# Down projection of a transformer layer, second phase: the last five inner steps done product by product, with their split weights kept in free slots

## The chip, the cores and the metric

The kernel runs on one core of one Trainium2 chip. The metric is device time in microseconds (us) of one execution. The kernel before was timed three times; its median is 942.09 us (941.8 to 942.45).

## The reference

One layer on 512 tokens of width 1024: a gated mixer of four branches, cross attention to 256 memory tokens, and a convolutional feed-forward part. The change touches the last matrix product, the down projection of the feed-forward part, and the place where its weights are prepared:

```python
def conv_ffn(h, w_up, conv_w, conv_b, w_down):
    up = causal_dwconv(h @ w_up, conv_w, conv_b)
    g, val = jnp.split(up, 2, axis=-1)
    return (jax.nn.gelu(g) * val) @ w_down          # (512 x 2816) @ (2816 x 1024)

    h = rms_norm(x, g[5])
    y = conv_ffn(h, ffn_w_up[l], ffn_conv_w[l], ffn_conv_b[l], ffn_w_down[l])
    x = x + rms_norm(y, g[6])                       # the layer's output
```

## The kernel before

All products are done in float32 precision by splitting each operand into a rounded high part and a low part: three matmuls (high by high, high by low, low by high) in `mm3`, lines 127 to 130. So every weight tile is loaded by SP's queue into a `raw` buffer (4 of them, used in turn), cast on ACT into `whi` (line 75) and subtracted on DVE into `wlo` (line 76), in `load_unit`. There are 4 buffers each of `whi` and `wlo`; a cast into one waits until PE has read what was in it four units earlier. `prefetch` keeps such units two ahead of their use. `unit_kept` does the same split into general slots (70 tiles of 128x512, handed out by `get` and returned by `put`), so that the split weights stay as long as wanted and wait for no `whi` buffer; a unit of 1024 columns takes two casts and two subtractions of 512 columns there.

The down projection is done as a 2 by 2 block product with seven products in place of eight. Token blocks are the two halves of the 512 tokens (each two tiles of 128), and the inner dimension is split in two halves of 11 tiles; an **inner step** i takes tile i of each half. The block sums of `w_down` that this needs are made on the chip earlier: `sums_load` (line 637) loads four quarters of one step on POOL's queue, `sums` (line 644) adds them on DVE and stores them to `wsum` in HBM. These run every third step of the gate loop (line 663 on), and the last two in the loop for the keys (`kT`, lines 800 to 803).

The down projection has two phases. The first (line 1081 on) runs four of the seven products over 11 steps; the second (line 1126 on) runs the other three, here called p3, p7 and p4 by the names of their PSUM banks, each for two token tiles. In the second phase a step needs two weight units: `wb` (512 columns of `w_down`, called **b** below, with the step's number) for p3, and `wz` (1024 columns of `wsum`, called **z**) for p7 and p4. A step is 3 products by 2 token tiles by 3 matmuls, 18 matmuls of 512 columns. For steps 0 to 8 the 18 matmuls are issued together. Steps 9 and 10 are held back and done **product by product**: p3 of tile 0 for both steps, then p3 of tile 1, then p7, then p4, and after each such block of 6 matmuls DVE and ACT finish what it made possible:

- after p3 of tile t: a subtraction (L1149), square and row sum on ACT (L724), gain (L1050), root (L732, L733), then `finish`: two scale-and-add (L1055) and two stores (L1056);
- after p7: a subtraction (L1154), a scale-and-add (L1155), square, gain;
- after p4 of tile t: an addition (L1159), square, gain, root, and `finish` of tile t + 2.

The operands of step i + 1 are made by `second_b` (line 1116) while step i runs. A list scheduler sets the order of each engine's instructions from the order of the program; each engine then works in order.

Of the kernel before, what the change touches and what calls it, by code (L numbers as in the profile page):

```python
# [8 lines left out]
F32 = mybir.dt.float32  # L9
F32R = mybir.dt.float32r  # L10
# [6 lines left out]
P = 128  # L17
S = 512
# [8 lines left out]
LOOK = 2  # L27

# [10 lines left out]
def tile_trunk(ctx: ExitStack, tc: tile.TileContext, a: dict, out: bass.AP):  # L39
# [21 lines left out]
    def put(*ts):  # L61
        for t in ts:
            free.append(held.pop(id(t))[0])
# [32 lines left out]
    for i in range(NP):  # L96
        plan += [(a["w_down"][NP + i][:, S:2 * S], S), (wsum[NP + i], 1024)]
# [536 lines left out]

    quarters = {}

    def sums_load(i):
        q = [[get("wq") for _ in R2] for _ in R2]
        for r in R2:
            for c in R2:  # L640
                gpsimd.dma_start(q[r][c], a["w_down"][c * NP + i][:, r * S:(r + 1) * S])
        quarters[i] = q

    def sums(i):
        (b11, b12), (b21, b22) = quarters.pop(i)
# [4 lines left out]
        gpsimd.dma_start(wsum[i][:, 0:S], b11)  # L650
        gpsimd.dma_start(wsum[i][:, S:2 * S], b22)
        gpsimd.dma_start(wsum[NP + i][:, 0:S], b21)
        gpsimd.dma_start(wsum[NP + i][:, S:2 * S], b12)
        put(b11, b12, b21, b22)

# [3 lines left out]
    for ki, kb in enumerate(order):  # L659
        for m in range(KT):  # L660
# [46 lines left out]
    LO, HI = slice(0, 256), slice(256, S)  # L707
# [45 lines left out]
    yt = [[None, None] for _ in T4]  # L753
# [250 lines left out]
    def pair_up(i):  # L1004
        g0, g1 = g[2 * i], g[2 * i + 1]
        hi, lo = get("gh", F32R), get("gl", F32R)
        for j, t in enumerate((g0, g1)):
            c = slice(j * 256, (j + 1) * 256)
            scalar.copy(hi[:, c], t[:, LO])
            vector.tensor_tensor(lo[:, c], t[:, LO], hi[:, c].bitcast(F32), op=ALU.subtract)  # L1010
        vector.tensor_sub(g1[:, LO], g0[:, LO], g1[:, LO])
        vector.tensor_sub(g0[:, LO], g0[:, LO], g0[:, HI])
        vector.tensor_sub(g0[:, HI], g1[:, HI], g0[:, HI])
        vector.tensor_add(g1[:, LO], g1[:, LO], g0[:, HI])
        gp1[i] = (hi, lo)
# [30 lines left out]
    def down_post(t, c):  # L1046
        n5.square(yt[t][c], t, c)
        if c == (1 if t < 2 else 0):
            n5.add(t, t + 1)
        vector.tensor_tensor(yt[t][c], yt[t][c], g6[c], op=ALU.mult)  # L1050

    def finish(t):
        n5.root(t, t + 1)
        for c in range(2):
            vector.scalar_tensor_tensor(yt[t][c], yt[t][c], n5.col(t), xt[t][c], op0=ALU.mult, op1=ALU.add)  # L1055
            sync.dma_start(out[t][:, HALF[c]], yt[t][c])  # L1056
        put(*yt[t])


    def product(ps, x, off, w, first, last, ts=(0, 1)):  # L1060
        for t in ts:
            tt = slice(off + t * P, off + (t + 1) * P)
            mm3(ps[t], (x[0][:, tt], x[1][:, tt]), w, first, last)

    T2 = (0, 1)
    ops = {}

    def second_a(i):
        g0, g1 = g[2 * i], g[2 * i + 1]
        r = get("r2")  # L1070
        hi, lo = get("sh", F32R), get("sl", F32R)
        vector.tensor_add(r[:, HI], g0[:, LO], g1[:, HI])
        scalar.copy(hi[:, LO], g0[:, HI])
        scalar.copy(hi[:, HI], r[:, HI])
        vector.tensor_sub(lo[:, LO], g0[:, HI], hi[:, LO].bitcast(F32))
        vector.tensor_sub(lo[:, HI], r[:, HI], hi[:, HI].bitcast(F32))
        put(r)
        ops[i] = (hi, lo)

    p1, p2, p6, p5 = ([bank(tag, "dn") for _ in T2] for tag in "BBCA")  # L1080
    second_a(0)
    held_a = []
    for i in range(NP):
        wa, ws = unit(), unit()
        if i + 1 < NP:
            second_a(i + 1)
        f, l = i == 0, i == NP - 1
        todo = [(p1, gp1[i], 0, wa(0, S), f, l), (p2, gp1[i], 256, wa(S, 2 * S), f, l),
                (p6, ops[i], 256, ws(S, 2 * S), f, l), (p5, ops[i], 0, ws(0, S), f, l)]
        if i < NP - 2:  # L1090
            for p in todo:
                product(*p)
            put(*gp1[i], *ops.pop(i))
        else:
            held_a.append(todo)
    d0, d1 = [get("d0") for _ in T2], [get("d1") for _ in T2]
    for n in range(4):
        for t in T2:
            for todo in held_a:
                product(*todo[n], ts=(t,))  # L1100
        for t in T2:
            if n == 0:
                yt[t][0] = get("yt")
                scalar.copy(yt[t][0], p1[t])
            elif n == 2:
                vector.tensor_sub(d0[t], p6[t], yt[t][0])
                vector.tensor_add(yt[t][0], yt[t][0], p2[t])
                down_post(t, 0)
                if t == 0:
                    scalar.activation(warm, n5.ss[:, 0:1], AF.Sqrt, scale=0.0, bias=epsc)  # L1110
            elif n == 3:
                vector.tensor_sub(d1[t], d0[t], p5[t])
    for i in (NP - 2, NP - 1):
        put(*gp1[i], *ops.pop(i))

    def second_b(i):
        g0, g1 = g[2 * i], g[2 * i + 1]
        ah, al = get("sh", F32R), get("sl", F32R)
        bh, bl = get("sh", F32R), get("sl", F32R)
        scalar.copy(ah, g1)  # L1120
        vector.tensor_sub(al, g1, ah.bitcast(F32))
        scalar.copy(bh[:, LO], g0[:, LO])
        vector.tensor_sub(bl[:, LO], g0[:, LO], bh[:, LO].bitcast(F32))
        put(g0, g1)
        ops[i] = (ah, al), (bh, bl)

    p3, p7, p4 = ([bank(tag, "dn") for _ in T2] for tag in "BBC")
    second_b(0)
    held_b = []
    for i in range(NP):  # L1130
        wb, wz = unit(), unit()
        if i + 1 < NP:
            second_b(i + 1)
        f, l = i == 0, i == NP - 1
        ga, gb = ops[i]
        todo = [(p3, ga, 0, wb(0, S), f, l), (p7, gb, 0, wz(S, 2 * S), f, l), (p4, ga, 256, wz(0, S), f, l)]
        if i < NP - 2:
            for p in todo:
                product(*p)
            put(*ga, *gb)  # L1140
        else:
            held_b.append(todo)
    for n in range(3):
        for t in T2:
            for todo in held_b:
                product(*todo[n], ts=(t,))
            if n == 0:
# [93 lines left out]
```

## Time and profile before

| | |
|---|---|
| median of 3 runs | 942.09 us |
| the profiled execution's own time | 941.86 us |
| its span, first to last instruction | 940.0 us |
| PE (matmul) busy | 922.4 us, 98% |
| DVE busy | 606.7 us, 65% |
| ACT busy | 441.1 us, 47% |
| chain that ended last | PE 94%, DVE 3%, ACT 2% |

The table is read from the bottom: the chain of work that ended last is PE's for 94% of the span, so that in most places only fewer matmuls or fewer gaps between them would shorten the time. The 3% of DVE and 2% of ACT say that somewhere PE is not what is waited for.

### The profile page before, as it was taken

What the parts mean: (1) busy time and instruction counts of PE and PEld (TensorE: products, weight loads), DVE (VectorE), ACT (ScalarE), POOL (GpSimd) and SP (SyncE); (2) the same over time, 40 slices, a digit from 0 to 9 for tenths busy, and PEclk for the clock granted to TensorE, in tenths of its full rate; (3) what the DMA queues carried; (4) which work ended last, traced back from release to release, by engine and by line L of the source; (5) the groups of instructions that cost most, each with busy time, mean ns of one, the idle gap of its engine ahead of it and who ended that gap; (6) DMA issues with size and microseconds to landing.
All of it is one profiled execution on the core that took longest, in us unless ns stands there. A gap on an engine that the chain in (4) does not pass through costs nothing.

```text
span 940.0 us, 12070 instructions
## 1 busy us (share of the span) xinstructions
PE 922.4 (98%) x4534; PEld 776.9 (83%) x4534; DVE 606.7 (65%) x940; ACT 441.1 (47%) x707; POOL 56.0 (6%) x117
## 2 busy tenths in 40 slices
PE   8999999999999999999999999999999999999994
PEld 7888888888888888889888888988888888888883
DVE  5877569645665566757544845486666666697847
ACT  7836336422342233456433737453443443465642
POOL 1100022401110000300000000000000000000000
PEclk9999999999999999999999999999999999999997
DMA  9432255835564524745522330133322322355552
GB/s 333 141 130 101 101 190 178 290 133 181 192 227 136 195 94 155 241 140 179 180 90 77 125 112 1 48 110 95 107 90 98 104 90 93 120 178 181 166 191 90
DMA packets 43563, 133.67 MB, mean 142 GB/s; under 512 B 6240, under 2 KB 7152, under 8 KB 43504
## 3 DMA queue, kind: packets, MB, share of 16 engines
q1 hardware_dynamic: 36288, 109.81, 35.5%
q0 software_dynamic: 7072, 23.09, 7.1%
q8 instruction: 35, 0.57, 0.2%
q14 instruction: 24, 0.20, 0.1%
q10 hardware_dynamic: 144, 0.00, 0.0%
HBM read 119.25 MB, written 13.63 MB: 141 GB/s over the span
## 4 chain that ended last, share of the span: by engine, by line
PE 94%; DVE 3%; ACT 2%; DMA 0%; issue 0%; SPq 0%; DVEq 0%; ACTq 0%
PE up L130 8%; PE up L128 8%; PE up L129 8%; PE gate L128 6%; PE gate L129 6%; PE gate L130 6%; PE win L128 4%; PE win L129 3%; PE win L130 3%; PE dn L129 3%; PE dn L128 3%; PE dn L130 3%; PE br L128 2%; PE mo L128 2%; PE q L128 2%; PE q L130 2%
## 5 line engine op out<-in xcount | busy, mean ns | idle before, releaser
L76 DVE TENSOR_TENSOR wlo<-raw,whi 128x1024 fp32r<-128x1024 f32 (+1 forms) x181 | 214.3, 1189 | 155.5 <-ACT whi L75 155.0
L75 ACT CAST whi<-raw 128x1024 fp32r<-128x1024 f32 (+1 forms) x181 | 185.1, 1026 | 276.0 <-issue 78.9
L128 PE MATMUL up<-h3h,whi 128*128 128x512 f32 (+1 forms) x368 | 138.2, 375 | 0.0
L129 PE MATMUL up<-h3l,whi 128*128 128x512 f32 (+1 forms) x368 | 138.1, 375 | 0.0
L130 PE MATMUL up<-h3h,wlo 128*128 128x512 f32 (+1 forms) x368 | 138.1, 375 | 0.0
L128 PE MATMUL gate<-xgh,whi 128*128 128x512 f32 x256 | 99.9, 390 | 0.0
L130 PE MATMUL gate<-xgh,wlo 128*128 128x512 f32 x256 | 99.7, 389 | 0.0
L129 PE MATMUL gate<-xgl,whi 128*128 128x512 f32 x256 | 99.6, 389 | 0.0
L129 PEld LDWEIGHTS up<-h3l,whi 128*128 128x128 f32 x368 | 69.3, 188 | 12.6
L128 PEld LDWEIGHTS up<-h3h,whi 128*128 128x128 f32 x368 | 69.3, 188 | 12.5
L130 PEld LDWEIGHTS up<-h3h,wlo 128*128 128x128 f32 x368 | 69.3, 188 | 12.3
L550 DVE SCALAR_TENSOR_TENSOR c<-up,par,c 128x511 f32<-128x511 f32 (+1 forms) x88 | 65.1, 745 | 1.3
L128 PE MATMUL win<-xgh,whi 128*128 128x512 f32 x144 | 57.2, 397 | 0.0
L128 PEld LDWEIGHTS gate<-xgh,whi 128*128 128x128 f32 x256 | 48.1, 188 | 10.0
L130 PEld LDWEIGHTS gate<-xgh,wlo 128*128 128x128 f32 x256 | 48.1, 188 | 10.0
L130 PE MATMUL win<-xgh,wlo 128*128 128x512 f32 x144 | 56.3, 391 | 0.0
L129 PEld LDWEIGHTS gate<-xgl,whi 128*128 128x128 f32 x256 | 48.1, 188 | 9.8
L129 PE MATMUL win<-xgl,whi 128*128 128x512 f32 x144 | 56.1, 390 | 0.0
L356 DVE TENSOR_TENSOR sg<-gate,rb0s 128x512 f32<-128x512 f32 x32 | 22.0, 688 | 44.5 <-PE gate L130 44.3
L128 PE MATMUL dn<-whi,sh 128*128 128x512 f32 x110 | 42.8, 389 | 0.0
L129 PE MATMUL dn<-wlo,sh 128*128 128x512 f32 x110 | 42.8, 389 | 0.0
L130 PE MATMUL dn<-whi,sl 128*128 128x512 f32 x110 | 42.8, 389 | 0.0
(376 smaller groups left out, 1736.3 us busy)
## 6 DMA issues: line engine op xcount, KB each, us to landing
raw<-in_w_up SPq DMA_DIRECT2D x44, 512.0 KB, 3.4
raw<-in_w_gate SPq DMA_DIRECT2D x32, 512.0 KB, 4.1
wq<-in_w_down POOLq DMA_DIRECT2D x44, 256.0 KB, 3.9
wsum<-wq POOLq DMA_DIRECT2D x44, 256.0 KB, 3.3
raw<-wsum SPq DMA_DIRECT2D x22, 512.0 KB, 3.6
raw<-in_w_in SPq DMA_DIRECT2D x18, 512.0 KB, 3.9
raw<-in_w_down SPq DMA_DIRECT2D x11, 512.0 KB, 4.3
raw<-in_w_br SPq DMA_DIRECT2D x8, 512.0 KB, 3.5
```

The lines of the kernel that those rows point to most:

```text
L75: scalar.copy(hi[:, :n], raw[:, :n])
L76: vector.tensor_tensor(lo[:, :n], raw[:, :n], hi[:, :n].bitcast(F32), op=ALU.subtract)
L128: tensor.matmul(ps, lhsT=w[0], rhs=x[0], start=first, stop=False)
L129: tensor.matmul(ps, lhsT=w[0], rhs=x[1], start=False, stop=False)
L130: tensor.matmul(ps, lhsT=w[1], rhs=x[0], start=False, stop=last)
L356: vector.tensor_tensor(t, ps, rb0s, op=ALU.mult)
L550: vector.scalar_tensor_tensor(dst[:, s:S], src[:, 0:S - s], pc(wname, (taps - 1 - s) * stride + off), dst[:, s:S], op0=ALU.mult, op1=ALU.add)
```

## The change

`HOLD = 5` steps of the second phase, 6 to 10 in place of 9 and 10, are held back and done product by product, so that a block has 15 matmuls. Their weights can't stay in the four `whi` buffers so long, so they are loaded by `unit_kept` into slots. `plan` ends 5 steps earlier; when step 5 is taken, the kept units of steps 6 and 7 are asked for, and each further step asks for one more. The two phases move into a function `seven`. The casts and subtractions of one small operand now share one slot (`sb`). The sums of `w_down` are started every second gate step from the sixth on, so that all 11 are done in the gate loop and none in the loop for the keys.

```diff
+HOLD = 5
-    for i in range(NP):
+    for i in range(NP - HOLD):
         plan += [(a["w_down"][NP + i][:, S:2 * S], S), (wsum[NP + i], 1024)]
...
+    def pair_b(g0, g1):
+        ah, al, b = get("sh", F32R), get("sl", F32R), get("sb", F32R)
+        scalar.copy(ah, g1)
+        vector.tensor_sub(al, g1, ah.bitcast(F32))
+        scalar.copy(b[:, LO], g0[:, LO])
+        vector.tensor_sub(b[:, HI], g0[:, LO], b[:, LO].bitcast(F32))
...
+    def seven(n, first, opa, opb, wua, wub, ha, hb, ready):
...
+            if i < n - hb:
+                for p in todo:
+                    product(*p)
+                put(ah, al, b)
+            else:
+                held.append(todo)
+                free_later += [ah, al, b]
+        for k in range(3):
+            for t in T2:
+                for todo in held:
+                    product(*todo[k], ts=(t,))
+                if k == 0:
+                    yt[t][1] = get("yt")
+                    vector.tensor_sub(yt[t][1], d1[t], bks[0][t])
+                    ready(t, 1, True)
...
+    def sums_step(load=True):
+        if len(summing) > 1 or (summing and not sumq):
+            sums(summing.pop(0))
+        if load and sumq:
+            summing.append(sumq.pop(0))
+            sums_load(summing[-1])
...
-            step = ki * KT + m - 5
-            if step >= 0 and step % 3 == 0:
-                sums_load(step // 3)
-            if step >= 2 and step % 3 == 2:
-                sums(step // 3)
+            if ki * KT + m >= 5 and (ki * KT + m - 5) % 2 == 0:
+                sums_step()
...
-        if m in (2, 4):
-            sums(8 + m // 2)
-        if m in (0, 2):
-            sums_load(9 + m // 2)
+        sums_step()
...
+    def w_second(i):
+        if i < NP - HOLD:
+            return unit(), unit()
+        b, ts = unit_kept(a["w_down"][NP + i][:, S:2 * S], S)
+        z, tz = unit_kept(wsum[NP + i])
+        kept_down[i] = ts + tz
+        return b, z
+
+    kept_at = ahead(lambda j: w_second(NP - HOLD + j), HOLD, 1)
+
+    def w_later(i):
+        if i >= NP - HOLD:
+            return kept_at(i - NP + HOLD)
+        w = w_second(i)
+        if i == NP - HOLD - 1:
+            kept_at(0)
+        return w
+
+    seven(NP, gp1, ahead(lambda i: pair_a(g[2 * i], g[2 * i + 1]), NP, 1),
+          ahead(lambda i: pair_b(g[2 * i], g[2 * i + 1]), NP, 1),
+          lambda i: (unit(), unit()), w_later, 2, HOLD, down_ready)
```

Three places show how the engines' orders move. First PE, right after the last matmul of step 5. Before (`dn_7395` and `dn_7396` are the banks of p3 for token tiles 0 and 1, `dn_7397` that of p7 for tile 0; `whi_7600` is b of step 6, `whi_7606` its z; `sh` and `sl` are the token operand):

```order
L128 MATMUL dn_7395<-whi_7600,sh_7611 128x512
L129 MATMUL dn_7395<-wlo_7601,sh_7611 128x512
L130 MATMUL dn_7395<-whi_7600,sl_7612 128x512
L128 MATMUL dn_7396<-whi_7600,sh_7611 128x512
L129 MATMUL dn_7396<-wlo_7601,sh_7611 128x512
L130 MATMUL dn_7396<-whi_7600,sl_7612 128x512
L128 MATMUL dn_7397<-whi_7606,sh_7613 128x512
```

Now, from the fourth held step on (`sv_7395` and `sv_7396` are p3 of tiles 0 and 1; `kwh` and `kwl` are the kept high and low parts: 7595 and 7596 of step 6, 7611 and 7612 of step 7, 7682 and 7683 of step 9, 7705 and 7706 of step 10):

```order
L129 MATMUL sv_7395<-kwh_7682,sh_7696 128x512
L130 MATMUL sv_7395<-kwl_7683,sh_7696 128x512
L131 MATMUL sv_7395<-kwh_7682,sl_7697 128x512
L129 MATMUL sv_7396<-kwh_7595,sh_7625 128x512
L130 MATMUL sv_7396<-kwl_7596,sh_7625 128x512
L129 MATMUL sv_7395<-kwh_7705,sh_7719 128x512
L131 MATMUL sv_7396<-kwh_7595,sl_7626 128x512
L129 MATMUL sv_7396<-kwh_7611,sh_7650 128x512
L130 MATMUL sv_7396<-kwl_7612,sh_7650 128x512
L130 MATMUL sv_7395<-kwl_7706,sh_7719 128x512
L131 MATMUL sv_7395<-kwh_7705,sl_7720 128x512
```

PE went from step to step and used each weight for two tiles at once; now it goes through p3 of tile 0 for steps 6 to 9, and the scheduler has put two matmuls of tile 1 ahead of step 10's first and three ahead of its second.

Second, ACT at the same place, from the last weight unit in a `whi` buffer (`whi_7563`, z of step 5) on. It was one cast of b and one of z per step; now (z of step 6 is `kwh_7601` and `kwh_7605`, of step 7 7617 and 7621, of step 8 7665 and 7669, of step 9 7688 and 7692; `sb_7721` and `sh_7696` are token operands):

```order
L665 CAST sh_7696<-c_6671 128x512
L76 CAST whi_7563<-raw_7562 128x1024
L118 CAST kwh_7601<-raw_7599 128x512
L118 CAST kwh_7605<-raw_7599 128x512
L118 CAST kwh_7611<-raw_7609 128x512
L118 CAST kwh_7617<-raw_7615 128x512
L118 CAST kwh_7621<-raw_7615 128x512
L118 CAST kwh_7659<-raw_7657 128x512
L118 CAST kwh_7665<-raw_7663 128x512
L118 CAST kwh_7669<-raw_7663 128x512
L118 CAST kwh_7682<-raw_7680 128x512
```

The kept casts stand in one run behind z of step 5, in the order of the steps.

Third, the end of DVE's order. Before:

```order
L1154 TENSOR_TENSOR d_925_7329<-d_925_7329,dn_7398 128x512
L1155 SCALAR_TENSOR_TENSOR d_923_7327<-d_923_7327,dn_7398 128x512
L1159 TENSOR_TENSOR d_922_7326<-d_922_7326,dn_7399 128x512
L1050 TENSOR_TENSOR d_925_7329<-d_925_7329,gain_6877 128x512
L1159 TENSOR_TENSOR d_923_7327<-d_923_7327,dn_7400 128x512
L728 TENSOR_TENSOR rs_n_6881<-ss_n_6880 128x1
L1050 TENSOR_TENSOR d_922_7326<-d_922_7326,gain_6876 128x512
L728 TENSOR_TENSOR rs_n_6881<-ss_n_6880 128x1
L1050 TENSOR_TENSOR d_923_7327<-d_923_7327,gain_6876 128x512
L733 RECIPROCAL rs_n_6881<-rs_n_6881 128x1 x2
L1055 SCALAR_TENSOR_TENSOR d_922_7326<-d_922_7326,rs_n_6881,xt_3157 128x512
L1055 SCALAR_TENSOR_TENSOR d_924_7328<-d_924_7328,rs_n_6881,xt_3158 128x512
```

Now (`sv_7399` and `sv_7400` are p4 of tiles 0 and 1, as `dn_7399` and `dn_7400` were):

```order
L739 TENSOR_TENSOR d_922_7326<-d_922_7326,sv_7399 128x512
L845 TENSOR_TENSOR rs_n_6881<-ss_n_6880 128x1
L1153 TENSOR_TENSOR d_922_7326<-d_922_7326,gain_6876 128x512
L850 RECIPROCAL rs_n_6881<-rs_n_6881 128x1
L1159 SCALAR_TENSOR_TENSOR d_922_7326<-d_922_7326,rs_n_6881,xt_3189 128x512
L1159 SCALAR_TENSOR_TENSOR d_924_7328<-d_924_7328,rs_n_6881,xt_3190 128x512
L739 TENSOR_TENSOR d_923_7327<-d_923_7327,sv_7400 128x512
L845 TENSOR_TENSOR rs_n_6881<-ss_n_6880 128x1
L1153 TENSOR_TENSOR d_923_7327<-d_923_7327,gain_6876 128x512
L850 RECIPROCAL rs_n_6881<-rs_n_6881 128x1
L1159 SCALAR_TENSOR_TENSOR d_923_7327<-d_923_7327,rs_n_6881,xt_3191 128x512
L1159 SCALAR_TENSOR_TENSOR d_925_7329<-d_925_7329,rs_n_6881,xt_3192 128x512
```

The finishing of the two last tiles was interleaved; now tile 2 is finished altogether before the addition that waits for PE's last block.

## Rows read from the trace of the kernel before

**Rows 1.** The page of the profile: busy time of the engines, and the chain that ended last by engine.

```profile
PE 922.4 (98%) x4534; PEld 776.9 (83%) x4534; DVE 606.7 (65%) x940; ACT 441.1 (47%) x707; POOL 56.0 (6%) x117
PE 94%; DVE 3%; ACT 2%; DMA 0%; issue 0%; SPq 0%; DVEq 0%; ACTq 0%
```

**Rows 2.** Busy time by stretches at the end; the columns are the stretch, its length, busy us and count of PE, PEld, DVE, ACT and POOL, the granted clock of TensorE as a share of full speed, the busy share of the DMA engines, GB/s.

```profile
900.00:920.00 20.00, 20.00 (x90) 16.58 (x89) 9.02 (x10) 8.12 (x10) 0.00 (x0) 1.00 0.46 156
...
926.00:928.00 2.00, 1.33 (x6) 0.76 (x5) 2.00 (x5) 0.00 (x0) 0.00 (x0) 1.00 0.70 262
928.00:930.00 2.00, 0.00 (x0) 0.00 (x0) 2.00 (x4) 0.45 (x1) 0.00 (x0) 1.00 0.71 262
930.00:932.00 2.00, 0.00 (x0) 0.00 (x0) 2.00 (x6) 1.05 (x5) 0.00 (x0) 0.60 0.00 0
932.00:934.00 2.00, 0.00 (x0) 0.00 (x0) 1.88 (x6) 1.14 (x4) 0.00 (x0) 0.50 0.00 0
```

**Rows 3.** The chain that ended last, where it leaves PE and its last piece: start us, us, what.

```profile
918.95 0.24 PE dn L130
...
919.21 1.06 ACT whi L75
920.30 1.22 DVE wlo L76
921.52 0.61 DVE yt L1149
...
934.98 1.32 DVE d L1055 x2
```

**Rows 4.** The last matmuls on PE in order of time: start us, us, engine, line, operation, out<-in.

```profile
926.49 0.39 PE L128 MATMUL dn<-whi,sh 128*128 128x512 f32 x1
...
926.95 0.39 PE L130 MATMUL dn<-whi,sl 128*128 128x512 f32 x1
```

**Rows 5.** DVE, ACT and SP's queue at the end in order of time (neighbours of one kind are merged, with their count); in brackets the idle time before and what ended it.

```profile
928.83 0.68 DVE L1154 TENSOR_TENSOR d<-d,dn 128x512 f32<-128x512 f32 x1
...
931.23 0.68 DVE L1159 TENSOR_TENSOR d<-d,dn 128x512 f32<-128x512 f32 x1
...
931.94 0.63 ACT L724 ACTIVATE sq<-d 128x512 f32<-128x512 f32 x1 [0.48 <-DVE d L1159]
...
932.70 0.16 DVE L728 TENSOR_TENSOR rs_n<-ss_n 128x1 f32<-128x1 f32 x1
...
933.38 0.21 DVE L733 RECIPROCAL rs_n<-rs_n 128x1 f32<-128x1 f32 x2
933.57 2.74 DVE L1055 SCALAR_TENSOR_TENSOR d<-d,rs_n,xt 128x512 f32<-128x512 f32 x4
934.35 2.32 SPq L1056 DMA_DIRECT2D out_y<-d  x4
```

**Rows 6.** ACT in the second phase in order of time: casts of 512 and 1024 columns.

```profile
888.14 0.62 ACT L75 CAST whi<-raw 128x512 fp32r<-128x512 f32 x1
888.66 0.62 ACT L1120 CAST sh<-c 128x512 fp32r<-128x512 f32 x1
...
894.73 1.05 ACT L75 CAST whi<-raw 128x1024 fp32r<-128x1024 f32 x1 [2.10 <-PE dn L130]
...
898.81 1.05 ACT L75 CAST whi<-raw 128x1024 fp32r<-128x1024 f32 x1 [2.10 <-PE dn L130]
...
919.21 1.05 ACT L75 CAST whi<-raw 128x1024 fp32r<-128x1024 f32 x1 [2.09 <-PE dn L130]
```

**Rows 7.** DVE in the second phase in order of time: two neighbouring subtractions of 512 columns.

```profile
883.61 0.68 DVE L76 TENSOR_TENSOR wlo<-raw,whi 128x512 fp32r<-128x512 f32 x1
884.22 0.68 DVE L1121 TENSOR_TENSOR sl<-c,sh 128x512 fp32r<-128x512 f32 x1
```

**Rows 8.** SP's queue in the second phase: the transfers of b of step 6, z of step 6 and b of step 7.

```profile
893.68 0.74 SPq L74 DMA_DIRECT2D raw<-in_w_down  x1
897.07 0.33 SPq L74 DMA_DIRECT2D raw<-wsum  x1
897.67 0.33 SPq L74 DMA_DIRECT2D raw<-in_w_down  x1
```

**Rows 9.** Transfers of `raw` tiles by issue, each line: what, count, KB each, us from issue to landing. First the spread of all from 880 to 925 us, then those issued from 886.9 to 889 us (two), then those issued from 888.9 to 890 us (two, while the others were under way).

```profile
DMA to landing us min/median/max: 2.7/3.4/4.3
...
raw<-wsum SPq DMA_DIRECT2D x1, 512.0 KB, 3.3
raw<-in_w_down SPq DMA_DIRECT2D x1, 256.0 KB, 3.3
...
raw<-wsum SPq DMA_DIRECT2D x1, 512.0 KB, 4.2
raw<-in_w_down SPq DMA_DIRECT2D x1, 256.0 KB, 4.3
```

**Rows 10.** The gate stage: DVE's addition of `w_down` quarters and the reading of a gate bank behind it, PE's first matmul that uses that bank again, and the stretch of the stage in which the DMA engines are fullest (columns as in Rows 2).

```profile
190.95 0.69 DVE L646 TENSOR_TENSOR wq<-wq,wq 128x512 f32<-128x512 f32 x1 [6.47 <-DMA wq<-in_w_down]
191.56 0.68 DVE L356 TENSOR_TENSOR sg<-gate,rb0s 128x512 f32<-128x512 f32 x1
...
194.06 0.39 PE L128 MATMUL gate<-xgh,whi 128*128 128x512 f32 x1
...
167.00:174.00 7.00, 7.00 (x35) 5.86 (x34) 5.57 (x8) 3.76 (x5) 2.89 (x6) 1.00 0.94 303
```

More of the change, by code (lines that the diff above doesn't have):

```diff
@@ new lines, in product @@
+    def product(ps, x, off, w, first, last, ts=T2):
+        for t in ts:
+            tt = slice(off + t * P, off + (t + 1) * P)
+            mm3(ps[t], (x[0][:, tt], x[1][:, tt]), w, first, last)
+    def seven(n, first, opa, opb, wua, wub, ha, hb, ready):
+        bks = [[bank(tag, "sv") for _ in T2] for tag in "BBCA"]
+        held, free_later = [], []
+        for i in range(n):
+            wa, ws = wua(i)
+            a, e = first[i], opa(i)
+            f, l = i == 0, i == n - 1
+            todo = [(bks[0], a, 0, wa(0, S), f, l), (bks[1], a, 256, wa(S, 2 * S), f, l),
+                    (bks[2], e, 256, ws(S, 2 * S), f, l), (bks[3], e, 0, ws(0, S), f, l)]
+            if i < n - ha:
+                for p in todo:
+                    product(*p)
+                put(*a, *e)
+            else:
+                held.append(todo)
+                free_later += [*a, *e]
+        d0, d1 = [get("d0") for _ in T2], [get("d1") for _ in T2]
+        for k in range(4):
+            for t in T2:
+                for todo in held:
+                    product(*todo[k], ts=(t,))
+            for t in T2:
+                if k == 0:
+                    yt[t][0] = get("yt")
+                    scalar.copy(yt[t][0], bks[0][t])
+                elif k == 2:
+                    vector.tensor_sub(d0[t], bks[2][t], yt[t][0])
+                    vector.tensor_add(yt[t][0], yt[t][0], bks[1][t])
+                    ready(t, 0, False)
+                elif k == 3:
+                    vector.tensor_sub(d1[t], d0[t], bks[3][t])
+        put(*free_later)
+        bks = [[bank(tag, "sv") for _ in T2] for tag in "BBC"]
+        held, free_later = [], []
+        for i in range(n):
+            wb, wz = wub(i)
+            ah, al, b = opb(i)
+            f, l = i == 0, i == n - 1
+            todo = [(bks[0], (ah, al), 0, wb(0, S), f, l), (bks[1], (b[:, LO], b[:, HI]), 0, wz(S, 2 * S), f, l),
+                    (bks[2], (ah, al), 256, wz(0, S), f, l)]
+            if i < n - hb:
+                for p in todo:
+                    product(*p)
+                put(ah, al, b)
+            else:
+                held.append(todo)
+                free_later += [ah, al, b]
+        for k in range(3):
+            for t in T2:
+                for todo in held:
+                    product(*todo[k], ts=(t,))
+                if k == 0:
+                    yt[t][1] = get("yt")
+                    vector.tensor_sub(yt[t][1], d1[t], bks[0][t])
+                    ready(t, 1, True)
+                elif k == 1:
+                    yt[t + 2][1] = d1[t]
+                    vector.tensor_sub(d1[t], d1[t], bks[1][t])
+                    vector.scalar_tensor_tensor(d0[t], d0[t], -1.0, bks[1][t], op0=ALU.mult, op1=ALU.add)
+                    ready(t + 2, 1, False)
+                else:
+                    yt[t + 2][0] = d0[t]
+                    vector.tensor_add(d0[t], d0[t], bks[2][t])
+                    ready(t + 2, 0, True)
+        put(*free_later)
@@ L1044, in tile_trunk, with down_ready @@
     n5 = TokNorm("n5")
-    def down_post(t, c):
+    def down_ready(t, c, last):
         n5.square(yt[t][c], t, c)
-        if c == (1 if t < 2 else 0):
+        if last:
             n5.add(t, t + 1)
         vector.tensor_tensor(yt[t][c], yt[t][c], g6[c], op=ALU.mult)
[L1052 to L1057, printed above, removed]
@@ L1060, in product @@
[L1060 to L1078, printed above, removed]
@@ L1080, in tile_trunk @@
[L1080 to L1127, printed above, removed]
@@ new lines, in down_ready, with ahead, at @@
+        if t == 0 and not last:
+            scalar.activation(warm, n5.ss[:, 0:1], AF.Sqrt, scale=0.0, bias=epsc)
+        if last:
+            n5.root(t, t + 1)
+            for h in range(2):
+                vector.scalar_tensor_tensor(yt[t][h], yt[t][h], n5.col(t), xt[t][h], op0=ALU.mult, op1=ALU.add)
+                sync.dma_start(out[t][:, HALF[h]], yt[t][h])
+            put(*yt[t])
+    def ahead(make, n, by):
+        made = []
+        def at(i):
+            while len(made) < min(n, i + 1 + by):
+                made.append(make(len(made)))
+            return made[i]
+        return at
@@ L1164, in _layout @@
+    seven(NP, gp1, ahead(lambda i: pair_a(g[2 * i], g[2 * i + 1]), NP, 1),
+          ahead(lambda i: pair_b(g[2 * i], g[2 * i + 1]), NP, 1),
+          lambda i: (unit(), unit()), w_later, 2, HOLD, down_ready)
+    for ts in kept_down.values():
+        put(*ts)
 def _layout(inp):
```

97 lines of the change are left out of this document (41 added, 56 removed).

## The prediction, as put on record before the changed kernel was run

> **What bounds the kernel now.** I first read the page [rows 1]: PE is busy for 98% of the span and is 94% of the chain that ended last, so a change that leaves the number of matmuls alone can gain only where the chain leaves PE. Then the stretches at the end [rows 2]: PE has its last work between 926 and 928, the span ends at 940.0, and DVE is full in between. The chain [rows 3] leaves PE at 919.19, long before PE's last matmul, and goes through DVE to the end: that is the sign that DVE lags behind PE, for the chain doesn't come back to PE. The order of time [rows 4, 5] gives the sizes. The last matmul starts at 926.95 and ends at 927.34. The addition that needs it (L1159 of tile 1) starts only at 931.23, 3.9 us later, behind a subtraction of p7 (L1154, 928.83) whose block had ended two blocks earlier. So from PE's end the kernel takes 940.0 - 927.34 = **12.66 us**.
>
> **Why DVE lags, and what the change does to it.** A matmul starts 0.227 us after the one before (926.49 to 926.95 in two steps, [rows 4]). A held block of two steps is 6 matmuls, 1.36 us. DVE's large operations of 512 columns come 0.61 us apart [rows 7], four scale-and-adds take 2.74, 0.69 each, and the small ones about 0.1 each [rows 5]. So what follows a block costs DVE: for p3 and p4 two operations, two small ones and two scale-and-adds, 2 x 0.61 + 0.2 + 2 x 0.69 = 2.8 us; for p7 three operations, 1.8 us. Each is more than 1.36, so the backlog grows to the end. With five steps a block is 15 matmuls, 3.40 us, more than either. DVE then keeps up, and behind the last matmul there is left only what tile 1 of p4 needs.
>
> **The new tail.** From the rows of the last tile [rows 5]: addition start to first scale-and-add start, 2.34 us, if nothing stands between (931.23 to 933.57, which holds square, row sum, root and reciprocal; another gain and a root of the other tile are in it already). Then two scale-and-adds, 1.37, and from their end to the span's end 940.0 - (933.57 + 2.74) = 3.69 for the stores. When does the addition start? DVE does the same chain for tile 0 just before, in its new order: 2.34 + 1.37 = 3.71 us from that addition, which could start 3.40 before PE's end; so 0.31 after PE's end. The tail is 0.31 + 2.34 + 1.37 + 3.69 = 7.71 us. **Gain: 12.66 - 7.71 = 4.9 us.** It can't be over 5.3, since only the 0.31 is a wait; it is smaller by as much as DVE still lags.
>
> **What the change gives back: weights that come late.** PE uses up a step in 18 x 0.227 = 4.08 us; the casts of z, which wait for PE's end of a step, show it: 894.73 is the end of step 2, 898.81 of step 3, 919.21 of step 8, so step 5 ends at 906.9 [rows 6]. From there PE now wants b of steps 6 to 10 within 2.72 us, where it wanted one step per 4.08. Slots are free, but the four `raw` buffers still pace the loading. I follow them, with casts of 512 columns at 0.62 (0.52 apart, so 1.15 for a kept z), of 1024 at 1.05, subtractions 0.61 apart, and a landing of 3.3 or 3.4, or 4.2 and 4.3 for the third and fourth of four transfers under way [rows 6, 7, 9]:
>
> - Up to z of step 6 and b of step 7 nothing moves: issued at 897.07 and 897.67 as before [rows 8].
> - z of step 5 goes into the last `whi` buffer after step 3, 898.81; in ACT's new order one operand cast (0.62) stands ahead. Cast to 900.45, subtraction (1.22, [rows 3]) to 901.7. This frees the buffer for z of step 7: issue 901.7, landing 905.0, two casts to 906.2, two subtractions to 906.9.
> - Behind it are issued b of step 8 (902.3), z of step 8 (903.0) and b of step 9 (903.6): four transfers in 2 us. z of step 8 lands at 907.2, b of step 9 at 907.9; cast to 908.95, subtraction, behind two of z, to 909.75.
> - z of step 9 follows the subtraction of z of step 7: issue 906.95, landing 910.35, casts to 911.5. b of step 10 is issued at 907.55, lands at 910.95, is cast behind z of step 9 to 912.05 and subtracted to 912.85.
>
> PE starts the held steps at 906.92. The ninth matmul is done at 908.96, the tenth at 909.19; the eleventh needs the low part of b of step 9, 909.75: **0.56 us** waited. Two more of step 9 and two of tile 1 that the scheduler moved ahead take it to 910.65; step 10's high part is there at 912.05: **1.4 us** waited. Four matmuls later its low part is there. Together 1.96, so **2.0 us** of stall, with 1.4 in one piece. Below it could be 0.5, with the 2.7 of the shortest landing in each link; above, with 4.3 for all three links of the chain (z of step 7, z of step 9, b of step 10), 2.0 + 2 x 0.95 = 3.9, since the last two overlap [rows 9].
>
> One rule speaks against the change here. The rows show the landing grow from 3.3 to 4.2 when four transfers are under way. The Trainium skill, DMA: Bandwidth & Descriptors, "Latency and other measured facts", says that the access time of HBM, which makes most of a transfer's fixed cost, grows with the load on it, from 0.2 us to 2 us. By it every kept transfer would be late, which is the upper end just given, and the gain 1.0; by the rows only the crowded ones are, and I go by the rows.
>
> **The other edits.** Five kept z are split in halves: one more cast and subtraction each, some 0.1 us on engines that are busy for 8.1 and 9.0 of 20 us there [rows 2]: nothing. The shared `sb` slot takes no instruction away. The sums of two more steps move into the gate stage: 8 additions, 8 loads and 8 stores on POOL's queue, out of a stage where PE hid them. In the gate stage PE hides them too, as long as DVE reads a gate bank before PE wants it: in the tightest place before, DVE waited 6.47 us for a quarter and read the bank until 192.2, 1.8 us before PE's matmul at 194.06 [rows 10]. I take nothing for it; without that cover it costs what the third rival says.
>
> **Sum.** 12.66 to 7.71 is -4.9, the stall +2.0: -2.9 against the profiled execution's 941.86, so 938.9. The median of 942.09 lies 0.2 above that execution: **939.2 us**. About 0.2%, 1.9 us, is what a measurement of this kernel can tell from no change, so faster means below 940.2. The bounds of the stall, 0.5 and 3.9, give 937.7 to 941.1 for this case.
>
> **Rivals.**
> 1. *No stall worth the name* (under 0.5 us). For it: the scheduler fills PE's wait with tile 1's matmuls. Against: three links of 5 us each from 898.8. Time 942.09 - 4.9 = 937.2, at most 0.5 more.
> 2. *Slower: the stall costs the clock.* The granted clock is 1.00 until 930, then 0.60 and 0.50, the lower of the two levels, 1.2 GHz, with PE idle since 927.34 [rows 2, 4]. Idle as long as that before step 10, the landings of z of step 9 and b of step 10 each some 1.7 late, would leave 15 matmuls or so at half rate: stall 0.6 + 3.1, then 15 x 0.227 = 3.4 more, less 4.9: +2.2, 944.3. It decides from there on; my 1.4 is under half of it. The Trainium skill, TensorE: Matmul & The Clock Gate, "Why this matters for your kernels", says to leave no idle gaps of that kind between bursts, since the clock then drops to half.
> 3. *The gate stage stalls.* The DMA engines are at 0.94 from 167 to 174 already [rows 10], and each wait of DVE for a quarter that is over 1.8 longer stops PE. Two such of 1 us: 941.2; it decides only where the loads bunch.
> 4. *DVE still lags*, for a reason that the order doesn't show: half of the 4.9 stays, 941.6.
>
> **How the numbers follow.** The forecast has 0.69; within it the stall is under 3.0 in about 8 of 10, so 0.55 faster, 0.14 same. Rival 1: 0.10, faster. Rival 2: 0.06, slower. Rival 3: 0.10 (0.01 faster, 0.07 same, 0.02 slower). Rival 4: 0.05 (0.02 faster, 0.03 same). Faster 0.68, same 0.24, slower 0.08. The range reaches from rival 1 with a tail 0.3 shorter, 936.9, to past rivals 3 and 4, 941.8.
>
> **What would show it.** Right: after PE's last matmul some 7.7 us to the span's end, the addition of the last tile within 0.4 us of it; DVE idle between blocks; PE with two gaps, at p3 of steps 9 and 10, of 2.0 us together, so its last matmul ends near 929.3. Wrong: DVE without gaps at the end; a gap over 3 us, or a clock below 1.00 before PE's end; a PE idle in the gate stage.

## The result, and the profile after

The changed kernel takes **945.01 us** (median of 9 runs, 944.28 to 947.08), the kernel before 942.45 in the same session: a ratio of 1.0029, with a 95% interval of 1.0019 to 1.0040. It is 2.6 us slower, where 2.9 us faster was forecast, and the time lies outside the range. The profiled execution has a span of 943.0 us, against 940.0.

The span of each kernel is cut at the same four places of the work: the start of PE's first matmul into a `win` bank, the start of its last high-by-high matmul into an `up` bank (the two down phases follow), the end of PE's last matmul, and the end of the span. The gate loop, a part of the second stretch, stands beside it (from the start of its first high-by-high matmul to that of its last, from the view of the tiles). All in us, of the profiled executions; e1 to e10 are the experiments below:

| kernel | to first `win` | `win` to last `up` | in it: the gate loop | to PE's end | tail |
|---|---|---|---|---|---|
| before | 31.7 | 790.1 | 221.5 | 105.5 | 12.7 |
| after | 32.3 | 796.6 | 226.8 | 106.7 | 7.4 |
| e1 old sums, 5 held | 33.3 | 790.1 | 221.5 | 106.9 | 7.3 |
| e2 before, new sums | 32.4 | 797.3 | 227.5 | 105.5 | 12.9 |
| e3 no additions | 33.3 | 802.6 | 234.0 | 107.0 | 7.3 |
| e4 sums start later | 32.4 | 795.4 | 226.9 | 106.9 | 7.4 |
| e5 additions on POOL | 31.8 | 794.7 | 226.1 | 107.0 | 7.9 |
| e6 old sums, 4 held | 31.7 | 790.0 | 221.5 | 105.7 | 8.1 |
| e7 old sums, 3 held | 32.9 | 790.1 | 221.5 | 105.5 | 9.1 |
| e8 old sums, 6 kept | 32.4 | 790.1 | 221.5 | 106.3 | 7.3 |
| e9 mixed rhythm, 4 held | 32.2 | 795.1 | 226.5 | 105.6 | 8.8 |
| e10 old sums, b first | 32.5 | 790.1 | 221.6 | 105.6 | 7.3 |

The first column varies by 1.6 us among kernels whose program there is the same, so it is taken as no effect of the change. What is left of the change reads off the first two lines: the tail is 5.3 shorter (4.9 forecast), the stretch to PE's end 1.2 longer (2.0 forecast), and the stretch ahead of it, for which nothing was forecast, is **6.5 us longer**: 1.2 before the gate loop and 5.3 in it.

The chain that ended last, by engine, answers to the second of [rows 1]: PE's share is 6 points lower than before, and a DMA has joined.

```profile
PE 88%; DVE 4%; DMA 3%; ACT 2%; issue 2%; POOL 0%; DVEq 0%; POOLq 0%; ACTq 0%
```

PE's waits over the whole span (line waited at, releaser: us in total, times, longest). Before there were two, 4.4 for `va` at the start and 0.2.

```profile
PE va L243 <- ACT xgh L257: 4.5, 1, 4.5
PE rbg L514 <- DVE rw L508: 2.7, 1, 2.7
PE win L129 <- DVE cv L625: 1.0, 1, 1.0
PE sv L129 <- ACT kwh L118: 0.4, 1, 0.4
PE kv L468 <- DVE st L455: 0.3, 1, 0.3
PE sv L130 <- DVE kwl L119: 0.2, 1, 0.2
```

The held group's waits are the two `sv` rows, 0.6 us. The large one, `rbg`, is at 170, far from the held group: a small matmul in which the second fiber of the gla branch spreads its norm (gla is one of the mixer's four branches; a fiber is a piece of its work that the program threads through the gate loop), and whose operand `rw` DVE makes from `rsg` by a reciprocal and a copy (L506, L508). Here is DVE's queue there, in order of time (in brackets the idle time before and what ended it); the additions of the sums are L757 to L760:

```profile
165.65 0.69 DVE L757 TENSOR_TENSOR wq<-wq,wq 128x512 f32<-128x512 f32 x1
...
168.78 0.69 DVE L760 TENSOR_TENSOR wq<-wq,wq 128x512 f32<-128x512 f32 x1
169.39 0.68 DVE L357 TENSOR_TENSOR sg<-gate,rb0s 128x512 f32<-128x512 f32 x1
171.03 0.69 DVE L758 TENSOR_TENSOR wq<-wq,wq 128x512 f32<-128x512 f32 x1 [0.96 <-DMA wq<-in_w_down]
171.64 0.19 DVE L506 RECIPROCAL rsg<-rsg 128x8 f32<-128x8 f32 x1
171.75 0.69 DVE L759 TENSOR_TENSOR wq<-wq,wq 128x512 f32<-128x512 f32 x1
172.36 0.42 DVE L508 COPY rw<-rsg 128x512 f32<-128x512 f32 x1
```

ACT had written `rsg` by 166.8 (first row below). DVE takes it up 4.8 us later: five additions that start after 166.8 and the reading of a gate bank (L357) stand ahead of it, and the last of the additions waits for its load; a sixth comes between the reciprocal and the copy. The chain of waits shows where that load was held up; start us, us, what:

```profile
166.55 0.27 ACT L505 ACTIVATE rsg<-hsum,epsc 128x8 f32<-128x8 f32 x1
```

```profile
166.03 0.54 POOL wsum L763
166.66 0.52 POOL wsum L761
167.18 3.83 DMA wq<-in_w_down
...
172.93 1.13 PE rbg L514 x8
```

The load was issued on POOL's queue behind two stores of sums, and took 3.83 us to land. PE, in order of time:

```profile
169.83 0.39 PE L129 MATMUL gate<-xgh,whi 128*128 128x512 f32 x1
172.93 1.13 PE L514 MATMUL rbg<-ident,rw 128*128 128x128 f32 x8 [2.71 <-DVE rw L508]
...
174.14 0.63 PE L131 MATMUL gate<-xgh,wlo 128*128 128x512 f32 x1
174.56 0.63 PE L129 MATMUL gate<-xgh,whi 128*128 128x512 f32 x1
...
177.54 0.39 PE L130 MATMUL gate<-xgl,whi 128*128 128x512 f32 x1
```

After the 2.71 us of idling, and the small `rbg` matmuls, the starts from 174.14 to 177.54 are 0.43 apart and not 0.23. The granted clock there (columns as in [rows 2]) is 0.50, the lower level of 1.2 GHz:

```profile
174.11:177.52 3.41, 3.41 (x9) 2.64 (x8) 2.87 (x5) 1.09 (x2) 2.40 (x5) 0.50 0.98 285
```

Set beside the kernel before, matmul by matmul, the gate loop's 5.3 us are 0.7 that were lost before this wait (0.6 of it at 150, where the wait for `kv` is), 2.9 for the wait, and 1.7 for the eight starts at the lower clock. The wait of 1.0 at 139 (`cv`) was followed by starts 0.23 apart. It has the same form, DVE's queue with a late load ahead of what PE needs:

```profile
138.63 0.69 DVE L757 TENSOR_TENSOR wq<-wq,wq 128x512 f32<-128x512 f32 x1 [4.16 <-DMA wq<-in_w_down]
139.24 0.69 DVE L625 TENSOR_TENSOR cv<-win,cv 128x512 f32<-128x512 f32 x1
```

The Trainium skill, TensorE: Matmul & The Clock Gate, "Why this matters for your kernels", says that long idle gaps between bursts bring the clock down to half; by these rows that holds for the gap of 2.71 and not for that of 1.0.

### The profile page after: what moved, and what is told of

It reads as the page before. It is cut to its first block, busy times and chain, and to the rows that moved or that the text cites. A ratio compares the mean times of both kernels' runs of the same rounds, so it can differ in the third digit from the quotient of the medians.

```text
span 943.0 us, 12047 instructions
## 1 busy us (share of the span) xinstructions
PE 926.1 (98%) x4534; PEld 778.0 (83%) x4534; DVE 607.0 (64%) x945; ACT 443.1 (47%) x713; POOL 55.5 (6%) x117
## 4 chain that ended last, share of the span: by engine, by line
PE 88%; DVE 4%; DMA 3%; ACT 2%; issue 2%; POOL 0%; DVEq 0%; POOLq 0%; ACTq 0%
PE up L131 8%; PE up L129 8%; PE up L130 8%; PE gate L131 6%; PE gate L130 6%; PE gate L129 6%; PE sv L129 3%; PE sv L131 3%; PE sv L130 3%; PE win L129 3%; PE win L131 3%; PE win L130 3%; PE mo L131 2%; PE q L130 2%; PE q L131 2%
## 5 line engine op out<-in xcount | busy, mean ns | idle before, releaser
L77 DVE TENSOR_TENSOR wlo<-raw,whi 128x1024 fp32r<-128x1024 f32 (+1 forms) x171 | 205.3, 1204 | 153.2 <-ACT whi L76 152.8
L76 ACT CAST whi<-raw 128x1024 fp32r<-128x1024 f32 (+1 forms) x171 | 176.9, 1036 | 252.9 <-issue 78.9
L129 PEld LDWEIGHTS gate<-xgh,whi 128*128 128x128 f32 x256 | 48.5, 189 | 10.2
L357 DVE TENSOR_TENSOR sg<-gate,rb0s 128x512 f32<-128x512 f32 x32 | 22.0, 688 | 39.1 <-PE gate L131 39.1
L1110 ACT ACTIVATE c<-c 128x512 f32<-128x512 f32 x22 | 13.9, 633 | 43.8 <-DVE c L551 43.8
L549 ACT ACTIVATE c<-up,par 128x512 f32<-128x512 f32 x44 | 33.7, 774 | 0.0
L129 PEld LDWEIGHTS win<-xgh,whi 128*128 128x128 f32 x144 | 27.0, 188 | 7.7 <-issue 2.1
```

What stands on the lines that cost most here:

```text
L76: scalar.copy(hi[:, :n], raw[:, :n])
L77: vector.tensor_tensor(lo[:, :n], raw[:, :n], hi[:, :n].bitcast(F32), op=ALU.subtract)
L129: tensor.matmul(ps, lhsT=w[0], rhs=x[0], start=first, stop=False)
L357: vector.tensor_tensor(t, ps, rb0s, op=ALU.mult)
L549: scalar.activation(dst, src, AF.Identity, bias=bias, scale=pc(wname, (taps - 1) * stride + off))
L1110: scalar.activation(cg, cg, AF.Gelu_apprx_tanh)
```

## Experiments

Each was timed beside the kernel before, with 4 to 12 runs of its own; the median of the kernel before was 942.3 to 942.6 us each time. The sums' code is named as in the changed kernel. Theory A: the loss is made in DVE's queue in the gate stage, where additions of the sums stand ahead of what PE waits for. The move of the sums holds three things at once: they start every second gate step and not every third, a sum's additions come four gate steps behind its loads and not two, and the last two sums leave the loop for the keys.

**e1, the old places of the sums.** Only the move of the sums is undone; the five held steps stay.

```diff
-            if ki * KT + m >= 5 and (ki * KT + m - 5) % 2 == 0:
-                sums_step()
+            step = ki * KT + m - 5
+            if step >= 0 and step % 3 == 0:
+                sums_load(sumq[step // 3])
+            if step >= 2 and step % 3 == 2:
+                sums(sumq[step // 3])
...
-        sums_step()
+        if m in (2, 4):
+            sums(sumq[8 + m // 2])
+        if m in (0, 2):
+            sums_load(sumq[9 + m // 2])
```

> The changed kernel with five held steps, but with the sums of w_down at the old places (every third gate step, the last two in the loop for the keys). Theory A (the loss sits in the gate stage: additions of the sums stand in DVE's queue ahead of the reciprocal of the second gla fiber, PE waits 2.7 us for rbg and then runs at the lower clock): PE is back at before's times up to the end of the up projection (821.8), only what the held group costs there (some 1.2 us) and gains in the tail (5.3 us) is left, so 942.4 - 4.1 = 938.3 us. Theory B (the loss comes with the held weights or the new function, and the wait at rbg is only where it shows): 944 to 945 us, as the change.

938.84 us, ratio 0.9958 (0.9945 to 0.9972). The stretch to the last `up` is that of before to the tenth, and DVE takes up the reciprocal at 166.98, 1.1 us after `rsg`. Without its move of the sums the change is worth -3.7 us. Theory B falls.

**e2, the new places alone.** The kernel before with the edit of e1 the other way round, two held steps.

```diff
-            if step >= 0 and step % 3 == 0:
-                sums_load(step // 3)
-            if step >= 2 and step % 3 == 2:
-                sums(step // 3)
+            if step >= 0 and step % 2 == 0:
+                if step >= 4 and step // 2 - 2 < NP:
+                    sums(step // 2 - 2)
+                if step // 2 < NP:
+                    sums_load(step // 2)
```

(The four lines in the loop for the keys go.)

> The kernel before with one edit: the sums of w_down every second gate step and all 11 in the gate loop, as in the change; two held steps as before. Theory A: the wait for cv at 139 (1.0 us), the wait for rbg (2.7 us) and the lower clock behind it come back in full, about 6.5 us: 942.4 + 6.5 = 948.9 us, with the tail of before, 12.7 us. Theory B: within 1 us of before, 942 to 943 us.

949.89 us, ratio 1.0076 (1.0063 to 1.0088): +7.3. The same two waits of PE:

```profile
PE rbg L513 <- DVE rw L507: 3.3, 1, 3.3
PE win L128 <- DVE cv L624: 1.1, 1, 1.1
```

e1 and e2 together: the move of the sums costs 7.3 alone and 945.0 - 938.8 = 6.2 on top of the held steps; the held steps give 3.7 alone and 949.9 - 945.0 = 4.9 on top of the move. The two add up to within 1.2 us.

**e3, no additions.** The four lines `vector.tensor_add(b11, b11, b12)` to `vector.tensor_add(b21, b21, b22)` are taken out of `sums`.

> The changed kernel without the four additions of each sum (so what is stored in wsum are the plain quarters, and the output is another one); the loads and stores of the sums stay, at the new places. Theory A (DVE's queue): no addition can stand ahead of the reciprocal, so the waits of PE for cv and rbg are gone: 945.0 - 6.5 = 938.5 us. Theory C (the traffic: 11 steps of loads and stores closer together delay the gate weights or what the fiber needs, and DVE only passes the delay on): PE still waits 2 us or more in the stretch 130 to 180, 943 to 945 us.

951.74 us, ratio 1.0091 (1.0076 to 1.0107). Neither expected time holds. Both waits of theory A are gone, as it says, and PE works without a gap from 100 to 189, with the DMA engines at 0.89 and 0.88 of their time in 160 to 180. Then it stops for 10.2 us. The chain there:

```profile
186.79 3.36 DMA wq<-in_w_down
190.16 7.26 DMA row<-in_mem_rows
...
198.24 0.94 ACT whi L76
```

Without the additions the scheduler puts the row norm of the memory (L212) early into ACT's queue, ahead of the cast of gate weights that PE needs, and its load comes late. So the run doesn't price the additions. It does show that in this order of the engines the traffic alone makes neither wait, and that a load waited for in an in-order queue can stop PE on another engine too.

**e4, the sums start three gate steps later.** `m >= 8 and (ki * KT + m - 8) % 2 == 0` in place of the fives.

> The changed kernel with the first sums three gate steps later (from the ninth gate step on, still every second one). In DVE's order the reciprocal of the second fiber then has the same number of additions ahead of it, but the one that waited for its load directly in front of the reciprocal is gone. If the wait for a load is what hurts (theory A in its narrow form): PE waits under 0.5 us for rbg, the clock stays, 938 to 940 us. If the mere number of additions ahead (seven of 0.6 us) hurts: PE still waits 2 us or more for rbg, 943 to 945 us.

943.84 us, ratio 1.0014 (1.0005 to 1.0024). Seven additions still stand ahead of the reciprocal from 164.9 on, none of them waiting for a load:

```profile
169.26 0.69 DVE L760 TENSOR_TENSOR wq<-wq,wq 128x512 f32<-128x512 f32 x1
...
170.47 0.19 DVE L506 RECIPROCAL rsg<-rsg 128x8 f32<-128x8 f32 x1
```

PE waits 1.56 us for `rbg` in place of 2.71, between the two expectations, and the granted clock stays at 1.00 there. So at this place the additions without a late load still cost up to 1.6; that the missing 1.1 is the late load is argued, since all that stands before it moved too. 1.5 and 0.4 are waited for `kv` at 150 instead, and 0.5 at 295, so the gate loop takes as long as in the change (226.9).

**e5, the additions on POOL.** `gpsimd.tensor_add` for the four `vector.tensor_add` in `sums`.

> The changed kernel with the additions of the sums issued on POOL in place of DVE; loads, stores and their places stay as in the change. Nothing of the sums can then stand ahead of the reciprocal in DVE's queue, while the traffic is kept. Theory A (DVE's queue): no wait of PE for cv or rbg, the gate stage takes as long as before (PE from the first gate matmul to the last 221.5 us, where the change has 226.8): 945.0 - 6.5 = 938.5 us. Theory C (traffic): PE waits 2 us or more in the stretch 130 to 180 for something that a load held up, 943 to 945 us.

944.44 us (12 runs, 939.72 to 950.35), ratio 1.0017 (1.0001 to 1.0033). The wait for `rbg` and that for `cv` are gone, and PE has no gap from 100 to 226, which is what theory A says of the place. The time is not got back: PE waits later, 2.0 us for `sg` at 228 and 283 and 1.4 for gate weights at 286, behind loads on SP's queue that waited for slots of the sums to come free. And the additions on POOL slow DVE down (DVE first, POOL below):

```profile
165.05 0.69 DVE L357 TENSOR_TENSOR sg<-gate,rb0s 128x512 f32<-128x512 f32 x1 [1.45 <-PE gate L131]
...
169.40 2.58 DVE L77 TENSOR_TENSOR wlo<-raw,whi 128x1024 fp32r<-128x1024 f32 x1 [0.19 <-ACT whi L76]
171.91 1.89 DVE L521 TENSOR_TENSOR sq<-sq,sg 128x512 f32<-128x512 f32 x1
...
177.20 1.21 DVE L77 TENSOR_TENSOR wlo<-raw,whi 128x1024 fp32r<-128x1024 f32 x1
```

```profile
164.88 1.30 POOL L757 TENSOR_TENSOR wq<-wq,wq 128x512 f32<-128x512 f32 x1 [0.75 <-DMA wq<-in_w_down]
...
169.59 1.30 POOL L759 TENSOR_TENSOR wq<-wq,wq 128x512 f32<-128x512 f32 x1
```

**e9, the new rhythm away from the fiber.** Four held steps; the sums of the first four steps at the old places, the other seven every second gate step, with the additions two gate steps behind the loads as in the kernel before, and not four as in the change.

```diff
+            if 0 <= step < 12 and step % 3 == 0:
+                sums_load(sumq[step // 3])
+            if 0 <= step < 12 and step % 3 == 2:
+                sums(sumq[step // 3])
+            if step >= 14 and step % 2 == 0:
+                sums(sumq[step // 2 - 3])
+            if 12 <= step <= 24 and step % 2 == 0:
+                sums_load(sumq[step // 2 - 2])
```

> Four held steps. The sums of the first four steps at the old places (every third gate step), the other seven every second gate step, so that all 11 are done in the gate loop as in the change, while DVE's order around the second gla fiber is that of before. If the change lost its time by what stands in DVE's queue at that fiber (theory A): the gate stage takes 221.5 us and the time is that of four held steps with the old places, 938.1 us. If the closer rhythm of the sums costs time anywhere in the gate stage: waits of PE after 200, 940 us or more.

944.42 us, ratio 1.0017 (1.0008 to 1.0026): theory A in its narrow form, that only the fiber is hurt, falls for this edit. No wait at the fiber, but a new one of 3.1 at 204.6, with starts 0.43 apart behind it up to 208.1, some 1.6 us more. DVE's queue ahead of it, and PE:

```profile
197.71 0.69 DVE L757 TENSOR_TENSOR wq<-wq,wq 128x512 f32<-128x512 f32 x1 [5.24 <-DMA wq<-in_w_down]
...
203.20 0.69 DVE L760 TENSOR_TENSOR wq<-wq,wq 128x512 f32<-128x512 f32 x1 [3.34 <-DMA wq<-in_w_down]
203.81 0.68 DVE L357 TENSOR_TENSOR sg<-gate,rb0s 128x512 f32<-128x512 f32 x1
```

```profile
204.64 0.63 PE L129 MATMUL gate<-xgh,whi 128*128 128x512 f32 x1 [3.10 <-DVE sg L357]
```

L357 is DVE's reading of a gate bank, and PE waits for that bank. The chain says why the load was late (start us, us, what):

```profile
189.83 6.52 DMA wsum<-wq
...
196.89 6.23 DMA wq<-in_w_down
```

This load was issued only when the store of an earlier sum had landed. The two took 6.5 and 6.2 us, with the DMA engines at 0.93 of their time from 160 to 200 (0.71 before). They are the long ones: from 100 to 340 the medians of such stores and loads are 3.7 and 4.5 us here, and 3.3 and 4.0 before. As the loads have two gate steps to land here and four in the change, e9 shows what the closer rhythm does with the old distance, not what it did in the change.

**e6 and e7, four and three held steps, old places of the sums.** `HOLD = 4`, `HOLD = 3` on e1.

> Old places of the sums, four held steps in place of five. Blocks of 12 matmuls, 2.72 us, against DVE's 2.8 behind p3 and p4: DVE just keeps up. PE starts the held group 4.1 us later, so the weights are there. If the 1.2 us that the held group of five loses are the late weights: the gap at p3 goes, the tail grows by 0.3 at most, 938.8 - 1.0 = 937.8 us. If they are something else (the order of the matmuls, other records): 938.8 to 939.2 us.

> Old places of the sums, three held steps. Blocks of 9 matmuls, 2.04 us, against 2.8 on DVE behind p3 and p4 and 1.8 behind p7: DVE falls behind by 0.76 in each of four blocks and gets 0.24 back in each of two. No gap at p3, a tail of 7.4 + some 1.0 to 1.8 = 8.4 to 9.2 us, 942.5 - 3.8 = 938.7 us. If DVE's lag does not depend on the block in this way (any hold over two is enough): a tail of 7.4 and 937.3 us.

938.12 us (ratio 0.9956, 0.9944 to 0.9968) and 939.13 us (0.9965, 0.9952 to 0.9978). PE has no gap in the held group, as reckoned, and the tail grows as blocks get shorter than DVE's 2.8 us: to 9.1 with three steps, as reckoned, and to 8.1 with four, 0.8 more than in e1 where 0.3 at most was expected. The times of e1, e6 and e7 lie within 1.0 us of one another and their intervals overlap, so their order rests on the table's last two columns, of one execution each: 114.2, 113.8 and 114.6 us together.

**e8, the weights of step 5 kept too.** The plan ends six steps early, `KEEP = 6` in place of `HOLD` in `w_second` and `w_later`; five steps are held.

> Old places of the sums, five held steps, and the weights of the step before them (step 5) loaded into slots too, so that z of step 5 waits for no whi buffer and the raw buffers behind it come free earlier. If the chain of raw buffers from z of step 5 on sets the 1.2 us that PE loses at p3: the chain starts up to 4 us earlier, no gap, 938.8 - 1.2 = 937.6 us. If only the landing of the transfers sets it: the gap stays at 0.7 or more and the time at 938.5 to 939 us.

938.03 us, ratio 0.9956 (0.9944 to 0.9968). One gap of 0.38 us is left, at the low part of b of step 10; the waits for step 9 are gone, and 0.6 of the 1.4 us that e1 takes more than the kernel before to PE's end are got back. The result lies between the two expectations: the chain from z of step 5 is a part of it and not all.

**e10, b before z.** The kept units of p3 first:

```diff
+            if i == NP - HOLD - 1:
+                for j in range(NP - HOLD, NP):
+                    bs.append(w_kept(a["w_down"][NP + j][:, S:2 * S], S))
+            return w
+        return bs[i - NP + HOLD], w_kept(wsum[NP + i])
```

> Old places of the sums, five held steps, and the kept units loaded in another order: b of steps 6 to 10 first, then z of steps 6 to 10 (before: b and z of a step, then the next). If late b of steps 9 and 10 is what PE waits for in the held group: no gap at p3, from the last matmul of the up projection to PE's end 105.5 us in place of 106.8, and with the tail of 7.4 us 938.8 - 1.2 = 937.6 us. If the number of transfers under way sets it: the gap moves to p7, where z of steps 9 and 10 is late, and the time stays at 938.5 to 939.5 us.

937.01 us, ratio 0.9941 (0.9929 to 0.9954), the lowest of all, though the interval overlaps those of e6 and e8. The waits of PE are those of the start alone:

```profile
PE va L243 <- ACT xgh L257: 4.5, 1, 4.5
PE sv L243 <- ACT svwh L271: 0.4, 1, 0.4
```

From the last `up` to PE's end it takes 105.6 us, as before the change. So the gaps of the held group were b of steps 9 and 10, late because units of z, not yet wanted, went ahead of them.

## Why the prediction was wrong

**The step that failed** stands under "The other edits": "I take nothing for it". It counted the sums as two steps more and covered them by one place, the tightest wait of DVE for a quarter before [rows 10]. What changed was the rhythm of all 11 sums and the distance from loads to additions, and with them DVE's order in the whole stage. The term is +6.5 us (1.2 + 5.3 in the table; e2 by itself +7.3), not 0. Without it the rest of the sum was near: -2.9 forecast, -3.7 in e1, where both the tail's gain and the stall came out better than reckoned.

**Two things were missed in that step.** First, only the gate banks were looked at as DVE's customers; the reciprocal of the gla fiber, `cv` and, in e5, `sg` wait in the same queue. The place of [rows 10], with 1.8 us to spare, was not the tightest. At the second fiber the kernel before has this, in order of time:

```profile
163.99 0.27 ACT L504 ACTIVATE rsg<-hsum,epsc 128x8 f32<-128x8 f32 x1 [0.33 <-PE hsum L502]
163.99 0.69 DVE L649 TENSOR_TENSOR wq<-wq,wq 128x512 f32<-128x512 f32 x1
...
165.62 0.43 DVE L507 COPY rw<-rsg 128x512 f32<-128x512 f32 x1
...
166.40 1.05 PE L513 MATMUL rbg<-ident,rw 128*128 128x128 f32 x8
```

`rw` was ready at 166.05 and PE took it at 166.40, 0.35 us later. Additions stood ahead of the reciprocal there too, but the last of them had begun when `rsg` was being written; in the change five begin after it. Second, rival 3 named the mechanism, DVE held up by a late quarter, but priced it at two waits of 1 us: 941.2. One wait of 2.7 brings the lower clock with it, which adds 1.7. Rival 2 had such a price, 15 matmuls at half rate or 3.4 us; no row gives the 15, and the rows behind this wait show eight starts at the lower clock. That rival expected it at the held group, where no gap was long enough.

**Rival 3's "only where the loads bunch" was too narrow.** At 139 DVE waited 4.16 us for a quarter, and PE 1.0 for `cv`, with the DMA engines at 0.56 of their time from 120 to 140. DVE's waits for quarters are 43.9 us in all in the change (16 waits) and 31.6 before (13); the longest is even shorter, 4.2 against 6.5. So the length of a wait alone does not decide; what stands behind it counts too. What is shown: the places of the sums cause the loss (e1, e2), and at the two waits additions on DVE ahead of PE's operands are where it acts (the rows above; e5: both waits go, traffic kept). What is open: which part of the 6.2 us is due to the number of additions and which to late loads, and which to the closer rhythm and which to the longer distance from loads to additions, for no run changes one of these two and keeps the other as in the change at the fiber.

**The tail was right.** It is 7.36 us (7.71 forecast). PE's last matmul starts at 935.25 and ends at 935.64; here it stands among DVE's instructions, with DVE's idle time:

```profile
932.28 0.69 DVE L739 TENSOR_TENSOR d<-d,sv 128x512 f32<-128x512 f32 x1 [1.17 <-PE sv L131]
...
935.25 0.39 PE L131 MATMUL sv<-kwh,sl 128*128 128x512 f32 x1
936.02 0.68 DVE L739 TENSOR_TENSOR d<-d,sv 128x512 f32<-128x512 f32 x1
...
938.42 1.41 DVE L1159 SCALAR_TENSOR_TENSOR d<-d,rs_n,xt 128x512 f32<-128x512 f32 x2
```

These answer to [rows 5]. DVE waits for PE before tile 0's addition, as forecast, and the last one starts 0.38 after PE's end (0.31 forecast; 3.9 before). To the scale-and-adds it is 2.40 (2.34). From their end, 939.83, to the span's end it is 3.17 us, where 3.69 was taken from [rows 5]: there four of them and four stores followed one another. So the gain was 5.3, not 4.9, and nearly all of the difference is this last term.

**The stall was at the right place and too large.** PE, in order of time:

```profile
916.54 0.50 PE L130 MATMUL sv<-kwl,sh 128*128 128x512 f32 x1 [0.23 <-DVE kwl L119]
...
918.10 0.50 PE L129 MATMUL sv<-kwh,sh 128*128 128x512 f32 x1 [0.36 <-ACT kwh L118]
```

The low part of b of step 9 and the high part of b of step 10, the two that were named; 1.2 us lost in all, where 2.0 was taken and 0.5 to 3.9 allowed. The held steps begin at 913.88. The first of the two is used 2.7 us later (2.8 forecast), the second 4.2 us later (5.1 forecast), so the last link was mis-sized: z of step 9 was issued at 912.05, 1.8 us before the held steps, where the forecast had it issued with them; its landing took 4.3 us and not 3.4. That late b of these steps is the cause is shown by e10. The granted clock stayed at 1.00 to 936, so rival 2 didn't come.

## What to carry to other kernels

When an edit moves filler work, such as sums done in the shadow of matmuls, look at every instruction that shares its queue and that the busy engine waits for, and at how much time each has to spare, not only at the place where the filler itself waits longest: an addition that waits for its load holds up all that stands behind it in order. A wait that brings the clock down costs more than its length: 1.7 us more after the 2.7 here, about as much (1.6) after the 3.1 of e9, and nothing after the 1.0 of the change or the 1.6 of e4. And load first what is wanted first: units of one step needn't be loaded together if the step is done product by product.

## What the runs showed of the hardware

Additions on POOL slow DVE's instructions with two operands in SBUF. In e5 a subtraction of 1024 columns took 2.58 us while POOL added (169.40), and 1.21 when it did not (177.20); a product of 512 columns (L521) took 1.89 in place of 0.69 (e4). Those with an operand in PSUM kept their time: L357 at 165.05 took 0.69 with a POOL addition under way from 164.88. The Trainium skill, SBUF — State Buffer, "Who interferes with whom", says that a DVE instruction with two inputs in SBUF contends with POOL instructions that read SBUF. The trace agrees. One POOL addition of 512 columns took mostly 1.30 us, twice DVE's 0.69. It can be POOL that is held up: at 161.78 DVE's subtraction of 1024 columns started 0.03 us ahead of a POOL addition and took its 1.22, and the addition took 2.31.
